# A ninth seven-product pair in half of one MLP, its operands kept in a quarter of the turned input, and one pass that adds by DMA

## The chip, the cores and the metric

The kernel runs on one core of one Trainium2 chip. The metric is the time of one execution on the device, in microseconds (us), as the median of several runs. The profile is of one further execution; its times are counted from the first instruction of its span. TensorE is called PE, its loading of the stationary operand PEld, VectorE DVE, ScalarE ACT, GpSimd POOL and SyncE SP, as in the profile.

## The reference, cut to what matters

Two layers work on 256 tokens of 2048 features in float32. The first layer mixes tokens with a convolution module, the second with latent attention; each is followed by the same kind of MLP, and a last RMSNorm ends the trunk:

```python
def sq_relu_mlp(h, w1, w2):
    return jnp.square(jax.nn.relu(h @ w1)) @ w2

for layer in range(DEPTH):
    ...
    h = rms_norm(x, norm_mlp_g[layer])
    x = x + sq_relu_mlp(h, mlp_w1[layer], mlp_w2[layer])
return rms_norm(x, final_norm_g)
```

`w1` is 2048 x 8192 and `w2` 8192 x 2048. The change is in the MLP of the first layer (`layer` 0) alone.

## The kernel before, in words

**Numbers in two parts.** Every float32 matrix is split into an upper part `hi` (a copy in float32r, by ACT) and a remainder `lo` (by DVE: the source minus `hi`), and a product is three matmuls: hi*hi, lo*hi, hi*lo (`mm3`, L202 to L204). Weights come in as tiles of 1 MB called `raw` (three buffers, loaded from SP's queue) and are split in halves of 128x1024, the upper part by L169 and the remainder by L173 for plain work, by L494 and L495 for mixed work. The results lie in tiles `hi` and `lo` with six buffers each (`WB`). So ACT and DVE can be ahead of PE by six half units of weights and no more.

**The MLP (`mlp`).** The hidden width is worked in two halves of 4096. In each half an up product makes eight groups of 512 hidden features (L650, L651, from the turned and normed input `xt`, four tiles of four 128-row blocks, each with its upper parts in one 256-column stretch and its remainders in the next). When a group's sums are complete, ACT and DVE square the rectified sums, scale them and split them into the tiles `sh`/`sl` or `gh`/`gl` (L668 to L682): two pairs of 128-row blocks a group, so 16 pairs a half, numbered 0 to 15. Then the down product runs through these 16 pairs twice, in two passes of 1024 output columns each (`for n in range(0, NNB, 2)`), into eight PSUM banks.

**Plain and mixed pairs.** A plain pair (`Sums.plain`) is a 2 x 2 block product with eight block products of three matmuls each, 24 matmuls of 512 columns. A mixed pair (`Sums.mixed`) uses the seven-product scheme of Strassen in Winograd's form, 21 matmuls, and pays for it with sums on DVE: on the weights in every pass (`mixed_weights`: L502, L503, L504 in place in `raw`, then 3584 elements a partition to split, in four pieces, instead of 2048 in two) and once on the hidden values (`mixed_inputs`, L515 to L525, into a tile of seven blocks of 128 columns for each part, called forms below). `MIXED` names the mixed pairs of each half: 0, 1, 4, 5, 8, 9, 12 and 13 in both halves of the first layer. Groups 0, 2, 4, 6 hold them, in tiles with room for seven blocks; groups 1, 3, 5, 7 are plain, in smaller tiles.

**A mixed pair in order.** PE takes block 1 of the upper weights (`b11`), `b21`, `b22`, then the summed forms `t1`, `t3`, `t4`, `t2`, three matmuls each. DVE makes the remainders of `b11` with `b21` (128x1024) and of `b22` (128x512), then L502, L503, L504, then the remainders of `t1` with `t3` and of `t4` with `t2` (128x1024 each). So the fourth product of a pair needs the third of the four pieces, and the sixth needs the last.

**The order of pairs** is set by hand in the loop over `i`: `HEAD` and `TAIL` spread the mixed pairs between the plain ones. With p for a plain pair and M for a mixed one, the first pass of the first layer's last half runs p p M M p M M p M p M M p M p p and the second p M p M p M M p M p M p M M p p. `Sums.join` adds the seven sums up before the last plain pair, and `Sums.close` adds the plain sums after it. `Sums.put` adds a finished block to the residual `xs`, on DVE (L577), or, where `by_dma` is set, through a DMA from POOL's queue that adds in place (L575); with `by_dma`, half of `close` is a copy by ACT (L601) and such a DMA too, the other half stays on DVE (L598). Before the change, `by_dma` is set in the first half of each layer and for the first pass of the second layer's last half; the first layer's last half adds all by DVE.

**Who orders the rest.** In the MLP the order of the instructions on each engine is made by the framework's planner when the kernel is built, from the program's order and its own estimate of times; the attention that follows (`manual_schedule`) keeps the order in which it is written. The first layer's last half ends in work for the next layer: in the middle of the last plain pair of its second pass, `prepare` turns the first two column blocks of `xs` into `xt[0]` and `xt[1]` (L266, L208, L215); the other two follow inside the attention.

Of the kernel before, what the change touches and what calls it, by code (L numbers as in the profile page):

```python
# [18 lines left out]
P = 128  # L19
# [3 lines left out]
S = T * P  # L23
# [18 lines left out]
WB = 6  # L42
LOOK = WB // 2 - 1
MIXED = {(layer, half): (0, 1, 4, 5, 8, 9, 12) + (13,) * (layer + half < 2) for layer in range(2) for half in range(2)}
N_MIXED = 4
HEAD, TAIL = (2, 1), 2

# [31 lines left out]
def trunk_kernel(  # L79
# [235 lines left out]
    at, cols = 0, []  # L315
# [8 lines left out]
    xt_cx, xt = [ExitStack()], []  # L324
# [184 lines left out]
    def mixed_inputs(v, fh, fl):  # L509

        def halves(src, at, n):
            hi, lo = fh[:, at : at + n, :], fl[:, at : at + n, :]
            nc.scalar.activation(hi, src, AF.Copy)  # L515
            nc.vector.tensor_tensor(lo, src, hi.bitcast(F32), op=ALU.subtract)

        a = v.rearrange("p k (t n) -> p (k t) n", t=T)
        a11, a21, a12, a22 = (a[:, i, :] for i in range(4))
        halves(a[:, 0:1, :], 0, 1)  # L520
        halves(a[:, 2:4, :], 1, 2)
        nc.vector.tensor_tensor(a22, a21, a22, op=ALU.add)
        nc.vector.tensor_tensor(a21, a11, a21, op=ALU.subtract)
        nc.vector.tensor_tensor(a11, a22, a11, op=ALU.subtract)
        nc.vector.tensor_tensor(a12, a12, a11, op=ALU.subtract)  # L525
        halves(a, 3, 4)
# [79 lines left out]
    def mlp(layer, ssq, next_gain, finish=None, before=None, beside=None, after_up=None):  # L606

        with ExitStack() as cx:
# [21 lines left out]

            for hf in range(HALVES):
                last = hf == HALVES - 1
                ms = MIXED[layer, hf]
                mixed = sorted({p // 2 for p in ms})
                plain = [g for g in range(ng) if g not in mixed]
                gs = {}
                for g in range(ng):
                    ps = [acc_tile() for _ in range(4)]
                    c0 = (hf * nkh + 4 * g) * P
                    for u in range(KC // 4):  # L640
                        if u == KC // 4 - 1:
                            step()
                        wj = load_split([rows(mlp_w1[layer], 4 * u, 4, c0, NB)], 4)
                        for j in range(4):
                            k = 4 * u + j
                            wh, wl = wj(j)
                            for b in range(4):
                                bs = slice(b * P, (b + 1) * P)

                                nc.tensor.matmul(ps[b], wh[:, bs], xhl(k), start=k == 0, stop=False)  # L650
                                nc.tensor.matmul(ps[b][:, :S], wl[:, bs], xh(k), start=False, stop=k == KC - 1)  # L651
                        step(6)
                    if hf == g == 0:
                        scales()
                    if beside is not None and g == 2:
                        beside(mp)
                        beside = None
                    if g in mixed or g in plain[len(plain) + len(mixed) - N_MIXED :]:
                        shape = [P, 2, 7, P] if g in mixed else [P, 4, S]
                        gs[g] = [mp.tile(shape, F32R, tag=f"s{c}", name=nm(f"s{c}"), bufs=N_MIXED) for c in "hl"]  # L660
                    else:
                        gs[g] = [mp.tile([P, 4, S], F32R, tag=f"g{c}", name=nm(f"g{c}"), bufs=ng - N_MIXED) for c in "hl"]
                    gh, gl = gs[g]
                    for b2 in range(2):
                        v = v_tile()
                        for b in range(2):
                            o = ps[2 * b2 + b]
                            nc.scalar.activation(v[:, b, :], o[:, S:], AF.Copy)  # L668
                            nc.vector.tensor_tensor(v[:, b, :], o[:, :S], v[:, b, :], op=ALU.add)
                        nc.vector.scalar_tensor_tensor(out=v, in0=v, scalar=0.0, in1=v, op0=ALU.max, op1=ALU.mult)  # L670
                        row = r2_row.rearrange("p (a n) -> p a n", a=1).broadcast_to([P, 2, S])
                        nc.vector.tensor_tensor(v, v, row, op=ALU.mult)
                        if 2 * g + b2 in ms:
                            mixed_inputs(v, gh[:, b2], gl[:, b2])
                            continue
                        if g in mixed:
                            v = v.rearrange("p k (t n) -> p (k t) n", t=T)
                            h, l = gh[:, b2, : 2 * T, :], gl[:, b2, : 2 * T, :]
                        else:
                            h, l = (a[:, 2 * b2 : 2 * b2 + 2, :] for a in (gh, gl))  # L680
                        nc.scalar.activation(h, v, AF.Copy)
                        nc.vector.tensor_tensor(l, v, h.bitcast(F32), op=ALU.subtract)  # L682
                nssq, add, prepare = residual_stage(last, next_gain)
                w, k_lo = mlp_w2[layer], hf * nkh
# [11 lines left out]
                due, rest = [], []  # L696

                def mixed_quad(sums, i):
                    g, b = divmod(ms[i], 2)
                    sums.mixed(w, k_lo + 4 * g + 2 * b, gs[g][0][:, b], gs[g][1][:, b], i == len(ms) - 1)  # L700

                split_end = last and finish is not None
                for n in range(0, NNB - 2 * split_end, 2):
                    sums = Sums(n, not last or split_end)
                    ks = [2 * p for p in ps]
                    at, head = 0, HEAD[n // 2]
                    for i, k in enumerate(ks):
                        upto = (len(ms) * (i - head + 1) + (head > 1) * (len(ks) - head - TAIL)) // (len(ks) - head - TAIL + 1)
                        while at < min(upto, len(ms)):
                            mixed_quad(sums, at)  # L710
                            at += 1
                        if i == len(ks) - TAIL + 1:
                            sums.join(room)
                        at_end = i == len(ks) - 1
                        sums.plain(
                            w, k_lo + k, hi, lo, k, at_end,
                            (lambda: [prepare(due.pop(0), out=room, rest=rest) for _ in range(len(due))]) if at_end else None,
                        )
                    sums.close(room)
                    while rest:  # L720
                        rest.pop(0)()
                    if last:
                        due += [n, n + 1]
                if last and not split_end:
                    put_off.extend(lambda n=n: prepare(n) for n in due)
                if split_end:
                    sums = Sums(NNB - 2, False)
# [25 lines left out]
    with ExitStack() as cx:  # L753
# [14 lines left out]
        b2 = cv.tile([P, D], F32, name="b2")  # L768
# [220 lines left out]
        with tc.manual_schedule():  # L989
# [99 lines left out]
            g = groups  # L1089
            upper_x, lower_x, last = ((0, 0),), ((0, 1),), ((1, 0),)  # L1090
# [828 lines left out]
```

## Time and profile before

| what | us |
|---|---|
| median of 3 runs (1935.26 to 1935.69) | 1935.29 |
| the profiled execution's own time | 1935.27 |
| its span, first to last instruction | 1933.5 |
| PE busy | 1919.0 |
| DVE busy | 1592.3 |
| ACT busy | 1095.5 |
| first layer, last half: up product | about 641 to 818.7 |
| its first pass of the down product | 818.7 to 900.3 |
| its second pass | 900.3 to 984.4 |

A row of the timeline gives the start, the time until the last of the merged instructions has ended, engine, line, operation, the tiles written and read, how many instructions were merged, and in brackets how long the engine sat idle before it and what ended that. Durations overlap: matmuls of 512 columns are recorded with 0.39 us each but start 0.2267 us apart (360 of them from 818.68 to 900.29). The same holds on DVE, where the next instruction starts a little before the end of the last. A wait row gives who waited for what, the sum in us, how often, and the longest.

### The profile page before, as it was taken

What the parts mean: (1) busy time and instruction counts of PE and PEld (TensorE: products, weight loads), DVE (VectorE), ACT (ScalarE), POOL (GpSimd) and SP (SyncE); (2) the same over time, 40 slices, a digit from 0 to 9 for tenths busy, and PEclk for the clock granted to TensorE, in tenths of its full rate; (3) what the DMA queues carried; (4) which work ended last, traced back from release to release, by engine and by line L of the source; (5) the groups of instructions that cost most, each with busy time, mean ns of one, the idle gap of its engine ahead of it and who ended that gap; (6) DMA issues with size and microseconds to landing.
All of it is one profiled execution on the core that took longest, in us unless ns stands there. A gap on an engine that the chain in (4) does not pass through costs nothing.

```text
span 1933.5 us, 28599 instructions
## 1 busy us (share of the span) xinstructions
PE 1919.0 (99%) x10805; PEld 1684.2 (87%) x10805; DVE 1592.3 (82%) x2464; ACT 1095.5 (57%) x1634; POOL 249.0 (13%) x208
## 2 busy tenths in 40 slices
PE   8999999999999999999999999999999999999998
PEld 8999888888888888888899998888888888888886
DVE  7999988877989777799976766877789887678898
ACT  5667755554555555555586655555555554455554
POOL 6999200000010100000001420000000010000000
PEclk9999999999999999999999999999999999999999
DMA  7766456665585866555665445465546686665674
GB/s 230 214 184 188 153 192 205 192 195 176 177 253 190 262 199 186 192 174 196 218 188 161 142 133 191 157 217 185 187 163 224 214 251 219 191 196 175 231 220 148
DMA packets 217756, 375.50 MB, mean 194 GB/s; under 512 B 16009, under 2 KB 91025, under 8 KB 217361
## 3 DMA queue, kind: packets, MB, share of 16 engines
q1 hardware_dynamic: 211968, 363.28, 58.2%
q0 software_dynamic: 4320, 7.87, 2.2%
q10 hardware_dynamic: 1328, 2.52, 0.4%
q8 instruction: 84, 1.38, 0.3%
q14 instruction: 56, 0.45, 0.1%
HBM read 363.68 MB, written 2.10 MB: 189 GB/s over the span
## 4 chain that ended last, share of the span: by engine, by line
PE 96%; DVE 2%; issue 0%; DMA 0%; ACT 0%; ACTq 0%; DVEq 0%
PE acc L650 24%; PE acc L202 15%; PE acc L204 15%; PE acc L203 15%; PE acc L651 13%; PE acc L818 8%; PE acc L1281 2%; DVE sum L905 1%; DMA xs<-in_x 0%; PE acc L1532 0%; PE acc L1555 0%; PE acc L1557 0%; PE acc L1556 0%; PE acc L1534 0%; PE acc L1533 0%
## 5 line engine op out<-in xcount | busy, mean ns | idle before, releaser
L173 DVE TENSOR_TENSOR lo<-raw,hi 128x1024 fp32r<-128x1024 f32 (+2 forms) x509 | 601.7, 1197 | 231.6 <-ACT hi L169 227.8
L169 ACT ACTIVATE hi<-raw 128x1024 fp32r<-128x1024 f32 (+2 forms) x574 | 583.9, 1036 | 358.4 <-PE acc L650 196.6
L650 PE MATMUL acc<-xt,hi 128*128 128x512 f32 x2048 | 710.5, 390 | 0.0
L651 PE MATMUL acc<-xt,lo 128*128 128x256 f32 x2048 | 577.5, 282 | 0.0
L650 PEld LDWEIGHTS acc<-xt,hi 128*128 128x128 f32 x2048 | 384.4, 188 | 80.6
L651 PEld LDWEIGHTS acc<-xt,lo 128*128 128x128 f32 x2048 | 387.1, 189 | 0.2
L494 ACT ACTIVATE hi<-raw 128x1024 fp32r<-128x1024 f32 x248 | 228.8, 949 | 234.8 <-DVE raw L502 137.6
L495 DVE TENSOR_TENSOR lo<-raw,hi 128x1024 fp32r<-128x1024 f32 x248 | 264.0, 1087 | 31.9 <-ACT hi L494 27.9
L202 PE MATMUL acc<-hi,sh 128*128 128x512 f32 x514 | 200.1, 389 | 0.0
L204 PE MATMUL acc<-lo,sh 128*128 128x512 f32 x514 | 200.1, 389 | 0.0
L202 PE MATMUL acc<-hi,gh 128*128 128x512 f32 (+1 forms) x516 | 200.0, 388 | 0.0
L203 PE MATMUL acc<-hi,gl 128*128 128x512 f32 (+1 forms) x516 | 199.9, 387 | 0.0
L204 PE MATMUL acc<-lo,gh 128*128 128x512 f32 (+1 forms) x516 | 199.9, 387 | 0.0
L818 PE MATMUL acc<-xt,hi 128*128 128x256 f32 x1024 | 180.1, 281 | 0.3 <-ACT b L1100 0.2
L203 PE MATMUL acc<-hi,sl 128*128 128x512 f32 x450 | 175.1, 389 | 0.0
L575 POOL DMA_DIRECT2D xs<-v x30 | 26.4, 972 | 1138.2 <-DVE lo L173 703.9
L905 DVE SCALAR_TENSOR_TENSOR sum<-ub,w_dw,sum 128x256 f32<-128x256 f32 x409 | 164.4, 484 | 3.5 <-ACT sum L875 3.0
L173 POOL TENSOR_TENSOR lo<-raw,hi 128x1024 fp32r<-128x1024 f32 x65 | 155.1, 2410 | 17.3 <-ACT hi L169 17.3
L818 PEld LDWEIGHTS acc<-xt,hi 128*128 128x128 f32 x1024 | 154.5, 188 | 1.1 <-ACT xt L1084 0.6
L818 PE MATMUL acc<-xt,lo 128*128 128x256 f32 x512 | 139.2, 279 | 0.0
L204 PEld LDWEIGHTS acc<-lo,sh 128*128 128x128 f32 x514 | 96.5, 188 | 20.5 <-DVE lo L495 0.3
L204 PEld LDWEIGHTS acc<-lo,gh 128*128 128x128 f32 x516 | 96.9, 188 | 19.9
(311 smaller groups left out, 2563.1 us busy)
## 6 DMA issues: line engine op xcount, KB each, us to landing
raw<-in_mlp_w SPq DMA_DIRECT2D x255, 1024.0 KB, 5.4
raw<-in_conv_w_pw SPq DMA_DIRECT2D x62, 512.0 KB, 5.0
raw<-in_conv_w_pw SPq DMA_DIRECT2D x16, 1024.0 KB, 5.0
raw<-in_mla_w_o SPq DMA_DIRECT2D x16, 1024.0 KB, 5.3
raw<-in_mla_w_kv_up SPq DMA_DIRECT2D x8, 1024.0 KB, 5.3
xs<-v POOLq DMA_DIRECT2D x30, 256.0 KB, 7.7
raw<-in_mla_w_in SPq DMA_DIRECT2D x8, 576.0 KB, 4.6
raw<-in_mla_w_in SPq DMA_DIRECT2D x4, 1024.0 KB
```

What stands on the lines that cost most here:

```text
L169: nc.scalar.activation(hi, raw[:, js, :], AF.Copy)
L173: eng.tensor_tensor(lo, raw, hi.bitcast(F32), op=ALU.subtract)
L202: nc.tensor.matmul(ps, sh, mh, start=start, stop=False)
L203: nc.tensor.matmul(ps, sl, mh, start=False, stop=False)
L204: nc.tensor.matmul(ps, sh, ml, start=False, stop=stop)
L494: nc.scalar.activation(hi, src, AF.Copy)
L495: nc.vector.tensor_tensor(lo, src, hi.bitcast(F32), op=ALU.subtract)
L650: nc.tensor.matmul(ps[b], wh[:, bs], xhl(k), start=k == 0, stop=False)
L651: nc.tensor.matmul(ps[b][:, :S], wl[:, bs], xh(k), start=False, stop=k == KC - 1)
L818: nc.tensor.matmul(pss[c][b][:, :S], w[i][:, bs], (xh, xl)[j](k), start=k == i + j == 0, stop=end and k == k0 + nk - 1 and (i, j) == terms ...
L905: nc.vector.scalar_tensor_tensor(out=out, in0=ubs[c][:, w : w + S], scalar=tap(c, w), in1=base, op0=ALU.mult, op1=ALU.add)
L1281: nc.tensor.matmul(ps2[b][t], x_kt(k, t), w[:, bs], start=k == g == i == 0, stop=k == KC - 1 and i == len(group) - 1,)
```

## The change

Pair 15 of the first layer's last half becomes a ninth mixed pair (`SPARE`). Its group, 7, has no tile with room for seven blocks, so its forms go to `xt[2]`, the quarter of the turned input that the half's up product has finished reading by then: two stretches of 896 columns. Both passes run p M p M M p M M p M M p M M p p, since `head` is 1 there. And `by_dma` is now set whenever `n == 0`, which differs from before in one place: the first pass of the first layer's last half.

```diff
+SPARE = {(0, 1): {15: 2}}
...
-                ms = MIXED[layer, hf]
+                ms, spare = MIXED[layer, hf], SPARE.get((layer, hf), {})
                 mixed = sorted({p // 2 for p in ms})
+                ms += tuple(spare)
+                forms = {}
...
-                        if 2 * g + b2 in ms:
-                            mixed_inputs(v, gh[:, b2], gl[:, b2])
+                        p = 2 * g + b2
+                        if p in spare:
+                            place = xt[spare[p]].rearrange("p a n -> p (a n)")
+                            forms[p] = [
+                                place[:, i * 4 * S : i * 4 * S + 7 * P].rearrange("p (f n) -> p f n", n=P) for i in range(2)
+                            ]
+                        elif p in ms:
+                            forms[p] = [gh[:, b2], gl[:, b2]]
+                        if p in ms:
+                            mixed_inputs(v, *forms[p])
                             continue
...
                 def mixed_quad(sums, i):
-                    g, b = divmod(ms[i], 2)
-                    sums.mixed(w, k_lo + 4 * g + 2 * b, gs[g][0][:, b], gs[g][1][:, b], i == len(ms) - 1)
+                    sums.mixed(w, k_lo + 2 * ms[i], *forms[ms[i]], i == len(ms) - 1)
...
-                    sums = Sums(n, not last or split_end)
+                    sums = Sums(n, not last or n == 0)
                     ks = [2 * p for p in ps]
-                    at, head = 0, HEAD[n // 2]
+                    at, head = 0, 1 if spare else HEAD[n // 2]
```

## The prediction

> **What bounds the kernel now.** First the page: shares of the engines, and the chain that ended last.
>
> ```profile
> span 1933.5 us, 28599 instructions
> ...
> PE 1919.0 (99%) x10805; PEld 1684.2 (87%) x10805; DVE 1592.3 (82%) x2464; ACT 1095.5 (57%) x1634; POOL 249.0 (13%) x208
> ...
> PE 96%; DVE 2%; issue 0%; DMA 0%; ACT 0%; ACTq 0%; DVEq 0%
> ```
>
> PE is never free for long, so over the whole kernel a matmul less is time less. But DVE at 82% is a mean over stages, and the change gives DVE more work in two passes. So next comes the busy time by stretches: the two passes of the first layer's first half (478 on), then those of the last half, which the change touches. The columns are the stretch, PE, PEld, DVE, ACT, POOL, the granted clock, the DMA share and GB/s.
>
> ```profile
> 478.00:560.00 82.00, 82.00 (x363) 67.90 (x363) 77.33 (x85) 45.75 (x53) 3.65 (x4) 1.00 0.60 196
> 560.00:641.00 81.00, 81.00 (x359) 67.06 (x358) 73.29 (x77) 46.10 (x51) 5.23 (x6) 1.00 0.69 219
> ...
> 818.70:900.30 81.60, 81.60 (x363) 67.58 (x362) 78.90 (x88) 45.17 (x52) 0.10 (x1) 1.00 0.56 188
> 900.30:981.80 81.50, 81.50 (x368) 67.51 (x367) 77.00 (x86) 48.04 (x62) 0.14 (x1) 1.00 0.55 189
> ```
>
> In the touched passes PE is busy throughout, and DVE for 78.9 of 81.6 us and 77.0 of 81.5. ACT has over 33 us to spare in each, the DMA engines over 40%. The waits of PE from 818 to 985 are a single row, at the start of the attention:
>
> ```profile
> PE acc L202 <- DVE xt L215: 0.4, 1, 0.4
> ```
>
> So both engines fit, with little left on DVE. How little is seen by the two timelines side by side. Mixed pairs are counted from M0 in each pass. On PE: the first matmul of the first pass, of its M2, of the plain pair after M3, and of the second pass.
>
> ```profile
> 818.68 0.39 PE L202 MATMUL acc<-hi,gh 128*128 128x512 f32 x1
> ...
> 844.53 0.39 PE L202 MATMUL acc<-hi,sh 128*128 128x512 f32 x1
> ...
> 854.05 0.39 PE L202 MATMUL acc<-hi,gh 128*128 128x512 f32 x1
> ...
> 900.29 0.39 PE L202 MATMUL acc<-hi,gh 128*128 128x512 f32 x1
> ```
>
> A pass is 8 x 21 + 8 x 24 = 360 matmuls in 81.61 us: **0.2267 us a matmul**, 5.44 a plain pair, 4.76 a mixed one (844.53 to 854.05 is two mixed: 9.52). M3 starts at 844.53 + 4.76 = 849.29 and needs t1's remainder nine matmuls later, at 851.33. On DVE at that time:
>
> ```profile
> 834.18 2.52 DVE L495 TENSOR_TENSOR lo<-raw,hi 128x1024 fp32r<-128x1024 f32 x2
> ...
> 840.62 1.22 DVE L502 TENSOR_TENSOR raw<-raw 128x1024 f32<-128x1024 f32 x1
> ...
> 847.38 1.22 DVE L502 TENSOR_TENSOR raw<-raw 128x1024 f32<-128x1024 f32 x1
> ...
> 849.97 2.52 DVE L495 TENSOR_TENSOR lo<-raw,hi 128x1024 fp32r<-128x1024 f32 x2
> ...
> 856.42 1.22 DVE L502 TENSOR_TENSOR raw<-raw 128x1024 f32<-128x1024 f32 x1
> ```
>
> The row at 849.97 is M3's last two pieces; the first ends 1.23 us on (2.52 for two that overlap), at 851.2. **The slack is 0.1 us.** And L502 to L502 is DVE's price: 840.62 to 847.38, 6.76 us for a mixed pair alone; 847.38 to 856.42, 9.04 for a mixed and a plain one, so 2.28 for the plain one. Two mixed and a plain pair cost DVE 15.80 us and PE 66 x 0.2267 = 14.96: in such a triple **DVE falls 0.84 us behind**. M1 (834.18: t1 there at 835.41, wanted at 829.57 + 4.76 + 2.04 = 836.37) had 1.0 of slack; one triple on, M3 has 0.1. The single mixed pairs between plain ones (9.04 on DVE, 45 x 0.2267 = 10.20 on PE) earn it back.
>
> **The change part by part.**
>
> *PE.* Pair 15 becomes mixed in two passes: 2 x 3 matmuls less, 6 x 0.2267 = **-1.36 us**. This is the whole direct gain. The Trainium skill ("TensorE: Matmul & The Clock Gate", Back-to-back issue gap) gives about 131 ns for a sustained matmul of 512 columns; by that it would be -0.79. The trace shows 0.2267 for float32r operands, and the measurement decides.
>
> *DVE, weights.* +6.76 - 2.28 = +4.48 us a pass, against 0.68 less of PE time.
>
> *DVE, forms.* Pair 15 gets `mixed_inputs` in place of one split. Costs by the spacing of the same instructions in group 6:
>
> ```profile
> 803.13 0.28 DVE L516 TENSOR_TENSOR sl<-v,sh 128x128 fp32r<-128x128 f32 x1
> 803.33 0.28 DVE L523 TENSOR_TENSOR v<-v 128x128 f32<-128x128 f32 x1
> 803.53 0.42 DVE L516 TENSOR_TENSOR sl<-v,sh 128x256 fp32r<-128x256 f32 x1
> 803.87 0.28 DVE L524 TENSOR_TENSOR v<-v 128x128 f32<-128x128 f32 x1
> ...
> 805.82 0.68 DVE L516 TENSOR_TENSOR sl<-v,sh 128x512 fp32r<-128x512 f32 x1
> 806.42 0.28 DVE L524 TENSOR_TENSOR v<-v 128x128 f32<-128x128 f32 x1
> ```
>
> 0.20 + 0.34 + 4 x 0.20 + 0.60 = 1.94, less the 0.60 of the 128x512 split that goes: +1.34 (by durations 2.50 - 0.68 = 1.82). It falls just ahead of the first pass, on the engine that is short. That the forms lie in `xt[2]` costs nothing: PE has read it by 818.6, before the last group's values exist, and its next writer is inside the attention.
>
> *DVE, sums.* In the first pass four puts and two of the four closing sums leave DVE: six instructions like these, 0.60 apart, **-3.6 us**, at the end of the pass. ACT gets two more copies, L601, of the size of L583's (L583's own is there already).
>
> ```profile
> 895.65 1.89 DVE L577 TENSOR_TENSOR xs<-v,xs 128x512 f32<-128x512 f32 x3
> ...
> L583 ACT ACTIVATE v<-acc 128x512 f32<-128x512 f32 x2 | 1.1, 574 | 0.0
> ...
> L575 POOL DMA_DIRECT2D xs<-v x30: 852/880/1308, 547.1 to 1846.7; - x30
> ...
>   DVE xs L598: 0.4, 1
> ...
> DMA to landing us min/median/max: 3.5/7.7/10.8
> ```
>
> POOL issues six DMAs of 256 KB, 0.88 us each; nothing else is queued on it then. The added wait: the first closing sum on DVE (L598, block 0) follows the landing of the DMA on the same block. The sum of the last plain pair but one takes PE some 10.9 us from the join, the landing 7.7 (at most 10.8), so it waits little (all 18 such sums of the trace waited 0.4 us together). Behind it on DVE would stand the next pass's weights, with slack by then (below). I take 0; bounds 0 and 1. The Trainium skill ("SBUF — State Buffer", SBUF: two separate sides) speaks against it: a DMA from GpSimd's queue has its descriptors written through a port that some DVE instructions lock, and waits until they end. Here the longest of 30 issues is 1.31 us, and the first of them run beside a DVE that is 94% busy (77.33 of 82), so the trace shows no such lock; by the rule the landing would be later, as in the rival "late adds".
>
> *The order.* M0 moves ahead of the second plain pair, so its pieces are wanted 5.44 us sooner, and the tail of the pass is a chain of four triples (p M M) instead of triples mixed with single pairs. Start of the first pass, DVE (with two ACT rows):
>
> ```profile
> 811.58 1.23 DVE L173 TENSOR_TENSOR lo<-raw,hi 128x1024 fp32r<-128x1024 f32 x1 [0.93 <-ACT hi L169]
> 814.37 1.23 DVE L173 TENSOR_TENSOR lo<-raw,hi 128x1024 fp32r<-128x1024 f32 x1 [1.56 <-ACT hi L169]
> 817.13 1.23 DVE L495 TENSOR_TENSOR lo<-raw,hi 128x1024 fp32r<-128x1024 f32 x1 [1.54 <-ACT hi L494]
> ...
> 828.71 2.96 DVE L495 TENSOR_TENSOR lo<-raw,hi 128x1024 fp32r<-128x1024 f32 x3 [1.21 <-ACT hi L494]
> ...
> 813.27 1.06 ACT L169 ACTIVATE hi<-raw 128x1024 fp32r<-128x1024 f32 x1 [1.72 <-PE acc L650]
> 816.04 1.06 ACT L494 ACTIVATE hi<-raw 128x1024 fp32r<-128x1024 f32 x1 [1.70 <-PE acc L650]
> ```
>
> Here DVE waits for ACT, and ACT for PE to free a buffer. M0's first pieces take the slots of the second plain pair (811.58 and 814.37), and L502 to L504, which need no new buffer, fit into the idle time behind them. So M0 is in time (wanted from 826.2 on), and of the 5.24 us idle in these four rows I count the last two, 1.54 + 1.21 = 2.75, as won; bounds 0 and 5.24.
>
> The balance: M2 now stands right behind M1 and wants t1 at 834.32 + 4.76 + 2.04 = 841.12. DVE has it at 835.41 + 6.76 + 1.34 - 2.75 = 840.76: slack 0.36. Three more triples cost 3 x 0.84 = 2.52, so PE waits **2.2 us** in the first pass (0 to 5.4 by the bounds, the latter with 1.82 and nothing won).
>
> Second pass: the last double today is
>
> ```profile
> 965.53 1.22 DVE L495 TENSOR_TENSOR lo<-raw,hi 128x1024 fp32r<-128x1024 f32 x1
> 966.66 0.68 DVE L504 TENSOR_TENSOR raw<-raw 128x512 f32<-128x512 f32 x1
> 968.56 1.23 DVE L495 TENSOR_TENSOR lo<-raw,hi 128x1024 fp32r<-128x1024 f32 x1 [1.21 <-ACT hi L494]
> ...
> 961.72 0.39 PE L202 MATMUL acc<-hi,sh 128*128 128x512 f32 x1
> ```
>
> PE starts the double at 961.72 and its second pair 4.76 later, wants that pair's t1 at 968.5 and has it at 966.75: 1.7 of slack. Up to this point the change takes 4.48 + 0.68 = 5.16 and gives 3.6 by the sums: 0.1 left. The last piece is only just in time already (wanted at 969.9, there at 969.79), because L504 came behind t1's remainder and DVE then waited 1.21 for ACT. I take 0.3 us of waiting; bounds 0 and 2.4 (twice 1.21).
>
> **Sum**: -1.36 + 2.2 + 0.3 = +1.1 us on the profiled execution's 1935.27, which is 0.02 below the median: **1936.4**. By the bounds -1.4 to +7.4 with the late sum's 1.
>
> **The rivals.** *DVE stays ahead.* If all idle time at the start is used, the first pass begins with over 2.5 us of slack and PE never waits: -1.36, 1933.9, no further down, as PE has no other wait there. For it: the 5.24 us idle. Against it: part of that idle is for buffers, which are as many as before. *The order of the pieces goes wrong.* The row at 968.56 shows 1.21 us of DVE idle when L504 is planned behind t1's remainder. With slack it is free; where DVE is already late it is lost. The first pass now has four doubles; if the planner does so at each, 4 x 1.21 = 4.8 comes on top: 1941.2, slower. It decides from the point where DVE's slack at M2 is under 0. Against it: at 849.97 (M3) the planner did not do so. *Late adds*: a landing of 10.8 after an issue behind another (0.9) or two holds DVE's first closing sum by 1 to 2 us, hidden by the slack between passes or not: 1936.4 to 1938. *The change does not act*, if the planner puts pair 15's forms so late that PE waits for them: the gain of 1.36 is spent there, 1935.3. Against it: pair 15 is the last mixed pair of the pass, some 65 us after its values exist.
>
> **Chances.** The forecast (waits of 1 to 4 us, so -0.4 to +2.6) 0.55; DVE stays ahead 0.27; wrong order 0.12; late adds and no effect 0.06. This kernel's measurement tells 0.2%, 3.9 us, from no change. The largest gain worked out is 1.4, so faster by more gets 0.02, for an order that changes elsewhere; slower by more gets the wrong order and a little of the forecast's tail, 0.12; the rest, 0.86, is within. The range leaves out the far part of the wrong order: 1933.8 to 1940.2.
>
> **What would show it.** Each touched pass has 357 matmuls; without waits they take 80.9 us. Right: waits of PE for DVE's L495 at the second pair of the doubles, growing along the first pass, DVE over 97% busy there, no L577 in that pass and six L575; the second pass nearly without waits. Wrong: no such waits (the first rival), DVE idle behind ACT inside the doubles (the second), or a wait of L598 for a landing.

## The result and the profile after

| kernel | median of 11 runs, us | range | ratio to before, 95% |
|---|---|---|---|
| before | 1935.4 | 1935.03 to 1936.19 | |
| changed | 1940.7 | 1939.03 to 1941.36 | 1.0025 [1.0016, 1.0035] |

The changed kernel is slower by about a quarter of a per cent. The forecast was 1936.4, and the median lies 0.5 above the top of its range. The profiled execution is the quickest of the eleven, 1939.03: on it, +3.8 us where +1.1 was forecast.

The page of the changed kernel, its first lines and the shares of the chain that ended last:

```profile
span 1937.3 us, 28629 instructions
...
PE 1920.1 (99%) x10799; PEld 1683.3 (87%) x10799; DVE 1599.0 (83%) x2474; ACT 1100.2 (57%) x1642; POOL 254.4 (13%) x214
...
PE 93%; DVE 5%; issue 1%; ACT 1%; DMA 0%; DVEq 0%; ACTq 0%
```

Six matmuls fewer, as meant, and a span 3.8 us longer. DVE's part of the chain grew from 2% to 5%. The page's mean share of DVE (82, now 83%) says nothing of this. The busy times of the two touched passes of the changed kernel do (columns as in the prediction):

```profile
819.00:901.60 82.60, 81.65 (x359) 66.86 (x358) 79.96 (x94) 48.16 (x57) 3.50 (x4) 1.00 0.61 197
901.70:984.60 82.90, 81.94 (x367) 67.03 (x366) 80.49 (x89) 50.65 (x66) 2.01 (x4) 1.00 0.63 199
```

DVE is busy for 97% of each, and PE, which was never without work here before, now has about a microsecond of gaps in each. The waits of PE in the changed kernel (who for whom, sum in us, how often, longest):

```profile
PE acc L205 <- DVE lo L496: 1.9, 4, 0.5
PE tr L267 <- DVE xt L216: 0.9, 2, 0.8
PE acc L205 <- DVE lo L174: 0.4, 1, 0.4
```

The first row is the wait that the prediction named, two in each pass. Such a wait counts from the end of the last record of 0.39 us; by the spacing of the starts each of the four costs PE 0.7 to 0.8 us. The other two rows stand at the start of the attention, where no loss was forecast.

To place the 3.8 us, both timelines of PE are cut at the same instructions: the first matmul of each pass, the first of the attention, and the first product after the attention's second set of turns.

| stretch | before | after | difference |
|---|---|---|---|
| up to the first pass | 818.68 | 819.03 | +0.35 |
| first pass | 81.61 | 82.62 | +1.01 |
| second pass, to the attention | 84.14 | 84.67 | +0.53 |
| start of the attention | 8.10 | 10.01 | +1.91 |

The sum is 3.80, and from there to the end the two timelines stay 3.8 apart. The 0.35 arises at the start of the kernel, ahead of anything that was edited. A pass now has 357 matmuls and saves 0.68; so the first pass waited 1.69 us and the second 1.21 more than before's. Before's second pass held some 0.7 us of waits itself, 0.5 of it at its end (the prediction's wait for L215, by the spacing of the starts), which the changed kernel does not have; so the changed second pass waited about 1.9 in all.

**First pass.** DVE in the changed kernel: L503 begins the sums of each mixed pair, the row at 839.38 is the last two pieces of M2, the L496 at 848.42 ends the sums of M3, the row at 856.76 is the last piece of M4, and the row at 871.26 is the two late pieces of M6.

```profile
839.38 2.52 DVE L496 TENSOR_TENSOR lo<-raw,hi 128x1024 fp32r<-128x1024 f32 x2
...
845.83 1.22 DVE L503 TENSOR_TENSOR raw<-raw 128x1024 f32<-128x1024 f32 x1
...
848.42 4.26 DVE L496 TENSOR_TENSOR lo<-raw,hi 128x1024 fp32r<-128x1024 f32 x4
...
856.76 1.23 DVE L496 TENSOR_TENSOR lo<-raw,hi 128x1024 fp32r<-128x1024 f32 x1 [0.35 <-ACT hi L495]
...
861.91 1.22 DVE L503 TENSOR_TENSOR raw<-raw 128x1024 f32<-128x1024 f32 x1
...
871.26 2.52 DVE L496 TENSOR_TENSOR lo<-raw,hi 128x1024 fp32r<-128x1024 f32 x2
...
877.70 1.22 DVE L503 TENSOR_TENSOR raw<-raw 128x1024 f32<-128x1024 f32 x1
```

861.91 to 877.70 is one triple (p M M): 15.79 us, forecast 15.80, against 14.96 for PE, and DVE has no idle time in it. The lead runs out at M6, and PE waits there and at M8. Two rows of PE's timeline after:

```profile
872.53 0.50 PE L205 MATMUL acc<-lo,sh 128*128 128x512 f32 x1 [0.51 <-DVE lo L496]
```

```profile
888.32 0.50 PE L205 MATMUL acc<-lo,xt 128*128 128x512 f32 x1 [0.44 <-DVE lo L496]
```

**Second pass.** At the turn of the passes, after: one of `join`'s sums and the last closing sum on DVE, then the next pass's first mixed weights.

```profile
893.47 0.68 DVE L587 TENSOR_TENSOR v<-acc,v 128x512 f32<-128x512 f32 x1
...
900.72 0.69 DVE L599 TENSOR_TENSOR xs<-acc,xs 128x512 f32<-128x512 f32 x1 [1.12 <-DMA xs<-v]
901.33 1.82 DVE L496 TENSOR_TENSOR lo<-raw,hi 128x1024 fp32r<-128x1024 f32 x2
```

And POOL's issue of the DMA that adds the block of L587:

```profile
894.55 0.86 POOL L576 DMA_DIRECT2D xs<-v  x1 [5.94 <-DVE v L587]
```

It lands 6.1 us after its issue, quicker than the 7.7 of the median before, and yet DVE stands idle for 1.12 us, since its closing sum on the same block was next. That is the second of the two closing sums on DVE; the first, on the block that ACT's copy feeds, did not wait. Weights for the next pass are queued behind it.

**Start of the attention.** Here the same instructions stand in another order. Before, DVE made the second of the two remainders of the attention's first weight tile (L173) between two closing sums, SP loaded the next tile into the buffer that this freed, and ACT made its upper part. Three views of before:

```profile
980.31 0.75 DVE L173 TENSOR_TENSOR lo<-raw,hi 128x576 fp32r<-128x576 f32 x1
```

```profile
981.09 0.37 SPq L1432 DMA_DIRECT2D raw<-in_mla_w_in  x1
```

```profile
986.16 0.69 ACT L169 ACTIVATE hi<-raw 128x576 fp32r<-128x576 f32 x1 [1.62 <-PE acc L203]
```

After, that remainder is the first of the four at 987.96, behind eight L216 (the six shown, two closing sums, and two more). DVE, SP, ACT and PE of the changed kernel:

```profile
983.58 2.49 DVE L216 SCALAR_TENSOR_TENSOR xt<-acc,vecs,xt 128x256 fp32r<-128x256 f32 x6
...
987.96 2.80 DVE L174 TENSOR_TENSOR lo<-raw,hi 128x576 fp32r<-128x576 f32 x4
```

```profile
988.78 0.37 SPq L1442 DMA_DIRECT2D raw<-in_mla_w_in  x1
```

```profile
992.68 0.69 ACT L170 ACTIVATE hi<-raw 128x576 fp32r<-128x576 f32 x1 [5.71 <-PE acc L204]
993.28 1.55 ACT L209 ACTIVATE xt<-tr,vecs 128x256 fp32r<-128x256 f32 x4
```

```profile
995.16 0.63 PE L267 MATMUL tr<-ident,xs 128*128 128x128 f32 x4 [0.75 <-DVE xt L216]
```

The load is issued right after the remainder in both kernels, 7.7 us later here. ACT waits 5.71 for it (the row names PE; but the load was issued 3.9 us before ACT went on, near the median of such loads on the page, here below).

```profile
raw<-in_mla_w_in SPq DMA_DIRECT2D x8, 576.0 KB, 4.4
```

ACT keeps the written order, so the copies of the turned input (L209) stand behind this wait, and PE waits for what follows from them. Of the 1.91 us, 0.62 are lost where PE waits for the late remainder itself (the L174 in its waits), before the first set of turns, and 1.29 after it.

### The profile page after: what moved, and what is told of

The parts are those of the page before. It is cut to its first block, busy times and chain, and to the rows that moved or that the text cites. A ratio compares the mean times of both kernels' runs of the same rounds, so it can differ in the third digit from the quotient of the medians.

```text
span 1937.3 us, 28629 instructions
## 1 busy us (share of the span) xinstructions
PE 1920.1 (99%) x10799; PEld 1683.3 (87%) x10799; DVE 1599.0 (83%) x2474; ACT 1100.2 (57%) x1642; POOL 254.4 (13%) x214
## 4 chain that ended last, share of the span: by engine, by line
PE 93%; DVE 5%; issue 1%; ACT 1%; DMA 0%; DVEq 0%; ACTq 0%
PE acc L653 24%; PE acc L205 14%; PE acc L203 14%; PE acc L204 14%; PE acc L654 13%; PE acc L828 8%; PE acc L1291 2%; DVE sum L915 1%; DVE lo L496 1%; DVE raw L503 0%; DVE lo L174 0%; PE acc L1542 0%; PE acc L1565 0%; PE acc L1566 0%; PE acc L1567 0%
## 5 line engine op out<-in xcount | busy, mean ns | idle before, releaser
L174 DVE TENSOR_TENSOR lo<-raw,hi 128x1024 fp32r<-128x1024 f32 (+2 forms) x505 | 597.1, 1197 | 230.0 <-ACT hi L170 226.1
L495 ACT ACTIVATE hi<-raw 128x1024 fp32r<-128x1024 f32 (+1 forms) x256 | 235.9, 949 | 234.4 <-DVE raw L503 142.6
L496 DVE TENSOR_TENSOR lo<-raw,hi 128x1024 fp32r<-128x1024 f32 (+1 forms) x256 | 272.2, 1087 | 28.9 <-ACT hi L495 24.6
L576 POOL DMA_DIRECT2D xs<-v x36 | 31.7, 973 | 1394.0 <-ACT v L584 962.6
L205 PE MATMUL acc<-lo,sh 128*128 128x512 f32 x514 | 200.5, 390 | 1.0 <-DVE lo L496 1.0
L203 PE MATMUL acc<-hi,gh 128*128 128x512 f32 (+1 forms) x500 | 193.8, 388 | 0.0
L205 PE MATMUL acc<-lo,gh 128*128 128x512 f32 (+1 forms) x500 | 193.7, 387 | 0.0
L204 PE MATMUL acc<-hi,gl 128*128 128x512 f32 (+1 forms) x500 | 193.7, 387 | 0.0
L174 POOL TENSOR_TENSOR lo<-raw,hi 128x1024 fp32r<-128x1024 f32 x65 | 155.2, 2415 | 17.6 <-ACT hi L170 17.6
L205 PEld LDWEIGHTS acc<-lo,sh 128*128 128x128 f32 x514 | 96.5, 188 | 22.7 <-DVE lo L496 2.6
L203 PEld LDWEIGHTS acc<-hi,sh 128*128 128x128 f32 x514 | 96.5, 188 | 19.8
```

What stands on the lines that cost most here:

```text
L174: eng.tensor_tensor(lo, raw, hi.bitcast(F32), op=ALU.subtract)
L203: nc.tensor.matmul(ps, sh, mh, start=start, stop=False)
L204: nc.tensor.matmul(ps, sl, mh, start=False, stop=False)
L205: nc.tensor.matmul(ps, sh, ml, start=False, stop=stop)
```

## The experiments

The standing theory at this point was the prediction's: DVE's rate in the triples is the bound. Against it stood the landing of the new DMA, the moved M0, something else in the ninth pair, and, for the help of a fourth engine, a conflict between POOL and DVE. Each run was timed in five rounds beside before (its medians there 1935.26 to 1935.51) and profiled once. Stretches are cut as above, in us; the landing column is the wait of DVE's closing sum for a DMA in the touched passes.

| run | median | ratio, 95% | first pass | second | attention | landing |
|---|---|---|---|---|---|---|
| before | 1935.4 | | 81.61 | 84.14 | 8.10 | none |
| changed | 1940.7 | 1.0016 to 1.0035 | 82.62 | 84.67 | 10.01 | 1.1 |
| e1 nine, DVE adds | 1940.9 | 1.0019 to 1.0043 | 82.72 | 85.47 | 10.47 | none |
| e2 eight, DMA adds | 1935.2 | 0.9991 to 1.0008 | 81.61 | 83.38 | 8.02 | none |
| e3 eight, M0 early | 1934.8 | 0.9990 to 1.0008 | 81.61 | 83.72 | 8.1 | none |
| e4 one pair lighter | 1938.4 | 1.0009 to 1.0027 | 82.25 | 86.20 | 8.09 | 2.6 |
| e5 single pair midway | 1938.0 | 1.0003 to 1.0020 | 82.59 | 85.26 | 8.02 | 1.7 |
| e6 nine pairs lighter | 1933.8 | 0.9985 to 1.0002 | 81.10 | 82.90 | 8.02 | none |
| e7 changed, again | 1939.5 | 1.0013 to 1.0033 | 82.59 | 85.59 | 10.05 | 2.1 |
| e8 landing avoided | 1935.9 | 0.9995 to 1.0012 | 82.74 | 83.41 | 8.1 | none |
| e9 POOL helps | 1946.8 | 1.0046 to 1.0072 | 85.81 | 90.93 | 8.23 | none |
| e10 all but the ninth | 1936.0 | 0.9994 to 1.0012 | 81.62 | 84.86 | 8.1 | none |
| e11 both passes by DMA | 1938.7 | 1.0011 to 1.0029 | 82.62 | 87.66 | 8.11 | 3.1 |
| e12 e8, lighter start | 1935.5 | 0.9992 to 1.0010 | 82.39 | 83.41 | 8.08 | none |

e2 and e3 leave the second pass's own work as it was and are 0.76 and 0.42 shorter there than before: they lack all or part of the waits that before has in its second pass. With one profile of most builds, a difference of that size in a second pass is not read.

**e1: the ninth pair, with the first pass added by DVE as before.**

```diff
-                    sums = Sums(n, not last or n == 0)
+                    sums = Sums(n, not last or split_end)
```

> The changed kernel with the sums of the first pass added by DVE again (nine mixed pairs, same order of pairs). Theory A (the ninth pair makes DVE the engine that PE waits for): DVE has six instructions of 0.60 us more, 3.6 us, at the end of the first pass; the first pass keeps its 1.7 us of waits, the second has 1.2 us plus most of the 3.6, so 1 to 3 us slower than the changed kernel, 1942 to 1944 us. Theory B (the add by DMA is the price, since DVE's first closing sums wait for its landing): the wait of 1.12 us goes and the time falls by about 1 us, to 1939.5.

It gave 1940.9, between what the two theories expected and the changed kernel's time within the interval: the second pass is 0.8 longer, the wait for a landing is gone, and the start of the attention takes 10.47. Both remainders of the attention's first weight tile stand behind the L216 here. PE loses most of the time by waiting for the second one directly; the late load is there too, and ACT's row names it, but after the first set of turns PE lost only 0.2:

```profile
PE acc L205 <- DVE lo L174: 2.0, 1, 2.0
```

```profile
993.86 0.69 ACT L170 ACTIVATE hi<-raw 128x576 fp32r<-128x576 f32 x1 [6.18 <-DMA raw<-in_mla_w_in]
```

So the DMA adds are not what made the kernel slow, and the 3.6 us that they take off DVE show in no median (1940.9 against 1940.7) and as 0.9 us in the two passes: part of what they gave went into the wait for their landing.

**e2 and e3: before, with only the DMA adds, and with only M0 moved ahead.**

```diff
-                    sums = Sums(n, not last or split_end)
+                    sums = Sums(n, not last or n == 0)
```

```diff
-                    at, head = 0, HEAD[n // 2]
+                    at, head = 0, 1 if (layer, hf) == (0, 1) else HEAD[n // 2]
```

> The kernel before with only the second half of the change: the first pass of the first layer's last half adds by DMA, eight mixed pairs in the old order. Theory A: DVE gets 3.6 us lighter where PE hardly waits, so nothing is won or lost: 1935.0 to 1935.6. Theory B: a closing sum waits 1 us or more for a landing and some of it reaches PE or the start of the attention: 1936.0 to 1937.5.

> The kernel before with only the earlier first mixed pair: the first pass of the first layer's last half takes the order of the second, p M p M p M M p M p M p M M p p, eight mixed pairs, sums by DVE. Theory A: no more work on DVE, so no more than some tenths of waits: 1935.2 to 1935.8. Rival C (the earlier place of the first mixed pair is the price, because its pieces come late): over 1 us more, from waits in the first two mixed pairs: 1936.5 or more.

Both tie with before, and PE is never idle in the touched passes (the first-pass and second-pass stretches of e2, then of e3):

```profile
819.00:901.60 82.60, 82.60 (x367) 68.40 (x366) 78.29 (x86) 46.08 (x54) 3.49 (x4) 1.00 0.61 196
901.70:984.60 82.90, 82.90 (x377) 68.95 (x377) 77.97 (x90) 51.42 (x68) 2.01 (x4) 1.00 0.63 201
```

```profile
819.00:901.60 82.60, 82.60 (x367) 68.47 (x366) 77.79 (x88) 46.74 (x54) 0.10 (x1) 1.00 0.56 191
901.70:984.60 82.90, 82.90 (x376) 68.83 (x374) 79.49 (x90) 49.92 (x66) 0.15 (x1) 1.00 0.59 192
```

Neither part costs anything alone. With DVE not short, the DMAs of e2 land in time.

**e10: everything but the ninth pair.**

```diff
-SPARE = {(0, 1): {15: 2}}
+SPARE = {}
...
-                    at, head = 0, 1 if spare else HEAD[n // 2]
+                    at, head = 0, 1 if (layer, hf) == (0, 1) else HEAD[n // 2]
```

> The changed kernel without the ninth pair: eight mixed pairs, both passes of that half in the order p M p M p M M p M p M p M M p p, the first pass adding by DMA. Theory A: DVE is 4.5 us a pass lighter than with nine, no triple follows another, so PE hardly waits and the time is that of the kernel before or some tenths less: 1934.3 to 1935.5. If the DMA or the order together cost what each alone did not, 1936 or more.

1936.0, a little above what was expected and not different from before; first pass 81.62, attention 8.1. So the loss comes with the ninth pair.

**e6: nine pairs, each with less DVE work.** L504 and L505, the last two weight sums of a pair, are left out in all nine pairs of both passes.

```diff
...
-        nc.vector.tensor_tensor(low[:, 1, :], low[:, 1, :], top[:, 0, :], op=ALU.subtract)
-        nc.vector.tensor_tensor(low[:, 0, :], low[:, 0, :], low[:, 1, :], op=ALU.subtract)
+        if sums:
+            nc.vector.tensor_tensor(low[:, 1, :], low[:, 1, :], top[:, 0, :], op=ALU.subtract)
+            nc.vector.tensor_tensor(low[:, 0, :], low[:, 0, :], low[:, 1, :], op=ALU.subtract)
...
```

> The changed kernel in which every mixed pair of the first layer's last half leaves out the second and third of its sums on the weights (L504, L505 there), so part of the product is not computed: a triple p M M costs DVE 15.8 - 2 x 1.33 = 13.1 us, less than PE's 15.0; matmuls, buffers and loads are the same. Theory A sharpened: what was lost in every triple is gone, so no waits in the doubles (under 0.3 in both passes) and none at the start of the attention: 1933.5 to 1935. Rival D (the six buffers by themselves make PE wait in the doubles, whatever DVE does): waits of 0.5 us or more stay at the second pairs of the doubles: 1937 to 1939.

Its two stretches:

```profile
819.00:901.60 82.60, 82.60 (x366) 68.25 (x365) 69.82 (x77) 47.25 (x57) 3.49 (x4) 1.00 0.64 204
901.70:984.60 82.90, 82.90 (x380) 68.99 (x380) 73.55 (x83) 52.76 (x71) 2.00 (x4) 1.00 0.65 207
```

DVE falls from 80 us to 70 and 74, and PE has no gap; 1933.8 is 1.6 below before (the interval still holds no change), PE's saving of 1.36 as near as can be told. The ninth pair's forms in `xt`, its order and its buffers make PE wait for nothing; DVE's work does. (Without these sums a piece is also ready sooner; but as DVE has no idle time in the triple above, it is the amount of its work that binds there.) The landing wait and the late attention are gone too.

**e4: the same for one pair.** The three weight sums are left out for M1 alone, once in each pass.

```diff
...
-                    sums.mixed(w, k_lo + 2 * ms[i], *forms[ms[i]], i == len(ms) - 1)
+                    sums.mixed(w, k_lo + 2 * ms[i], *forms[ms[i]], i == len(ms) - 1, not (spare and i == 1))
```

> The changed kernel in which the second mixed pair of each pass leaves out its three sums on the weights (L503 to L505 there), so part of the product is not computed: DVE has 2.6 us less in each pass, PE the same 357 matmuls. Theory A: the slack at the doubles grows by 2.6 us and the waits of 1.7 and 1.2 us go below 0.4 together; with them gone the time is 1935.4 - 1.4 plus what the start of the attention keeps (0 to 1.9): 1934.0 to 1936.3. If DVE's work is not the cause (theory B, or the start of the attention by itself), it stays at 1938.5 to 1940.5.

This missed: 1938.4 lies just below what was expected if DVE's work were not the cause, and e6 was needed to tell. Early in the pass DVE was relieved of the sums of one pair (M3's take 2.59 us in the changed kernel, 845.83 to 848.42), and the first pass waited 1.32 in place of 1.69. DVE spent the rest of the relief at once, idle behind ACT (waits of e4's DVE over both passes, and the wait for a landing, which was longer):

```profile
DVE lo L496 <- ACT hi L495: 7.4, 7, 1.8
...
DVE xs L600 <- DMA xs<-v: 2.6, 1, 2.6
```

The same wait for ACT summed to 3.5 in the changed kernel.

**e7: the changed kernel once more**, for its spread between executions.

> The changed kernel once more, for a second profile: 1939 to 1941.4. If what differs between its executions is the landing of the added DMAs, DVE's closing sum waits a different time for it than 1.12 us and the second pass differs; if it is the start of the attention (a weight load that waits for DVE to free its buffer), the time from the first matmul of the attention to the end of its second turn differs from 10.0 us.

DVE in e7, the row that answers to 900.72 above:

```profile
901.26 0.69 DVE L599 TENSOR_TENSOR xs<-acc,xs 128x512 f32<-128x512 f32 x1 [2.09 <-DMA xs<-v]
```

The same instructions in the same order: 0.97 more of waiting for the landing, and a second pass 0.92 longer. With DVE this late, a wait of its own reaches PE nearly one for one.

**e5: the second pass with its single mixed pair in the middle** (p MM p MM p M p MM p MM p p).

```diff
+                        if spare and n:
+                            upto = (0, 2, 4, 5, 7, 9, 9)[i]
```

> The changed kernel with the second pass in the order p M M p M M p M p M M p M M p p: the single mixed pair stands in the middle instead of first, so no more than two of the triples p M M follow each other. Theory A, sharpened (in each such triple DVE needs 15.8 us and PE 15.0, and the six buffers of remainders cap the lead that DVE can carry into it, so each triple after the first costs PE up to 0.84 us): the second pass's waits fall from 1.2 us to under 0.6, the first pass keeps its 1.7; if the backlog at the end of the pass falls too, so do the waits at the start of the attention: 1936.5 to 1939.5. If only the total of DVE's work counts and not the order (no cap), the second pass is unchanged and the time stays at 1939.5 to 1941.

The second pass did not get shorter, 85.26; it carried a landing wait of 1.7, so whether the order of the pairs helps there was not shown. The time lies in the range that was expected, but not by the shorter second pass that was to bring it there: the kernel is quicker than the changed one by 2.7, and its profile has 2.0 of that in the attention, 8.02: with another order in the pass, the planner put two remainders ahead of the L216 again.

**e8: no closing sum behind a DMA.** Blocks of the first column are added by DVE in `join` (some 1.2 us of DVE), so the sums of `close` on DVE touch no block that a DMA adds to.

```diff
-            self.put(0, 0, a if self.by_dma else u1)
+            self.put(0, 0, a if self.by_dma and not dve0 else u1, dve0)
...
-                self.put(t, n, o)
+                self.put(t, n, o, dve0 and n == 0)
...
-                            sums.join(room)
+                            sums.join(room, bool(spare) and n == 0)
```

> The changed kernel in which the join of the first pass adds its two blocks of the first column by DVE, and only the other two by DMA: DVE has 1.2 us more, but its closing sums touch no block that a DMA adds to. If the landing of the added DMA (1.12 and 2.09 us of DVE in two profiles) is a part of the loss by itself, the second pass's waits of PE fall by about 0 to 0.9 us and the spread between executions shrinks: 1938.5 to 1939.5. If DVE's time counts alone, 1.2 more against 1.1 to 2.1 less leaves it at 1939 to 1941. The start of the attention (1.9 us) should stay in both.

The closing sums of e8, and its second pass:

```profile
898.03 1.36 DVE L599 TENSOR_TENSOR xs<-acc,xs 128x512 f32<-128x512 f32 x2
```

```profile
901.70:984.60 82.90, 82.72 (x372) 68.06 (x370) 81.51 (x92) 51.75 (x70) 2.02 (x4) 1.00 0.62 197
```

More work for DVE (81.5 us, 98%) and fewer waits: a second pass of 83.41. In the builds in which DVE's closing sum waits for a landing (the changed kernel, e5, e7, e4) the second pass grows nearly one for one with that wait: 1.1, 1.7, 2.1 and 2.6 give 84.67, 85.26, 85.59 and 86.20 (e5's order and e4's sums differ from the others'). The time fell further than expected, to 1935.9, since the attention starts on time as well. The first pass still waits 1.81.

**e11: both passes add by DMA.**

```diff
-                    sums = Sums(n, not last or n == 0)
+                    sums = Sums(n, True)
```

> The changed kernel with the second pass adding by DMA too: DVE has 3.6 us less at the end of that pass, just before the attention. If the 1.9 us at the start of the attention come from DVE's backlog (the first attention weights' remainders late, so the buffer free late and the fourth load late), they go: 1937.0 to 1938.5, with the waits inside both passes as in the changed kernel. If the columns' landing makes the next layer's turning wait instead, 1940 or more.

The closing sum after the first pass, in e11:

```profile
904.02 0.69 DVE L599 TENSOR_TENSOR xs<-acc,xs 128x512 f32<-128x512 f32 x1 [3.10 <-DMA xs<-v]
```

The landing wait rose to 3.1 and the second pass to 87.66 (in an execution 2.7 above the median of its eleven, whose first pass began 1.3 later than the changed kernel's). The attention started on time, 8.11. As DVE has 3.6 us less to do just before it, this run alone does not tell a late DVE from a bad order; e4 and e5 do, whose second passes end later than the changed kernel's, with that pass's sums on DVE, and whose attention starts on time.

**e12: e8 with a lighter start.** ACT rectifies and squares the last group of hidden features, which takes 1.2 us off DVE at the start of the first pass.

```diff
...
-                        nc.vector.scalar_tensor_tensor(out=v, in0=v, scalar=0.0, in1=v, op0=ALU.max, op1=ALU.mult)
+                        if spare and g == ng - 1:
+                            nc.scalar.activation(v, v, AF.Relu)
+                            nc.scalar.activation(v, v, AF.Square)
+                        else:
+                            nc.vector.scalar_tensor_tensor(out=v, in0=v, scalar=0.0, in1=v, op0=ALU.max, op1=ALU.mult)
```

> The kernel without landings on DVE's blocks (the join of the first pass adds its first column by DVE) in which ACT, not DVE, rectifies and squares the last group's values: two instructions of 0.60 us less on DVE just ahead of the first pass, nothing else. If DVE's lead counts wherever it is won, the first pass's waits fall from 1.8 us by 1.2 to 0.6 and the time to 1934.6. If the six buffers cap the lead (as leaving 2.6 us out of the second mixed pair lowered the first pass's waits by 0.4 alone), the first pass keeps 1.3 to 1.8 us of waits and the time is 1935.3 to 1936.

The first pass waited 1.46, against 1.81 in e8. DVE spent the 1.2 us at once, idle behind ACT, where the same three instructions of e8 follow without a gap:

```profile
820.17 1.23 DVE L496 TENSOR_TENSOR lo<-raw,hi 128x1024 fp32r<-128x1024 f32 x1 [0.53 <-ACT hi L495]
...
822.75 1.23 DVE L174 TENSOR_TENSOR lo<-raw,hi 128x1024 fp32r<-128x1024 f32 x1 [0.42 <-ACT hi L170]
...
825.48 1.23 DVE L174 TENSOR_TENSOR lo<-raw,hi 128x1024 fp32r<-128x1024 f32 x1 [0.30 <-ACT hi L170]
```

DVE comes to the plain pair after M2 only 0.06 sooner than in e8, counted from the first matmul of the pass. The 0.35 arises later: at the last piece of M4 DVE waits 0.35 for ACT in e8, as at 856.76 in the changed kernel, and not in e12.

**e9: POOL makes the second remainder of three plain pairs a pass.**

```diff
-            at_j = split(load([rows(w, k, 2, self.n * NB, 2 * NB)], 2), nc.vector)
+            at_j = split(load([rows(w, k, 2, self.n * NB, 2 * NB)], 2), nc.vector, helper)
...
+                            nc.gpsimd if spare and 1 < i < 5 else None,
```

> The changed kernel in which POOL makes the second remainder (128x1024, 2.41 us on POOL elsewhere in the profile) of the plain pairs that stand between the doubles, three in each pass: DVE has 1.14 us less in each of these triples, 14.7 against PE's 15.0. Theory A: the waits in the doubles and at the start of the attention go and the time comes to 1934 to 1936. Rival E (POOL and DVE hold each other up while both read such tiles): DVE's or POOL's instructions get longer in these stretches and the time stays at 1938 or goes above 1941.

The slowest of all, 1946.8. A remainder on POOL in e9, and what DVE did beside it:

```profile
859.56 2.68 POOL L174 TENSOR_TENSOR lo<-raw,hi 128x1024 fp32r<-128x1024 f32 x1 [14.46 <-ACT hi L170]
```

```profile
860.47 3.46 DVE L496 TENSOR_TENSOR lo<-raw,hi 128x1024 fp32r<-128x1024 f32 x2 [0.49 <-ACT hi L495]
```

The same two pieces took DVE 1.82 in the changed kernel. POOL ends at 862.24, and 1.69 later DVE is done: it got next to nothing done in the 1.77 us beside POOL. The Trainium skill ("SBUF — State Buffer", SBUF: two separate sides) says that a DVE operation with two SBUF inputs and a GpSimd operation that reads SBUF exclude each other for the whole instruction; the rows agree.

## Why the prediction was wrong, step by step

*PE, -1.36: right.* e6, where nothing waits, gains 1.6 on before.

*DVE's price of a triple: right.* 15.79 measured.

*First pass, 2.2 of waits: right in kind, and 1.69 in size.* PE waits at the second pairs of the late doubles, as forecast, but from M6 on, where the forecast's balance has them from M4. The forecast had M2's t1 piece ready 0.36 us before it was wanted; in the changed kernel it was 1.3. Of that difference 0.45 is a misreading: the remainder of a weight enters only in the third of a product's three matmuls (PE's waits above are at L205), and the forecast counted to the first. With that corrected the sum gives 1.7. The other 0.5 is DVE earlier than forecast, and most of it goes again, 0.35, as DVE waits for ACT at M4. That the sum fits does not make slack a balance without a ceiling: ACT and DVE can be ahead by six half units and no more, so time won early is mostly spent idle behind ACT (e4: 0.4 of 2.6 us arrived; e12: 0.06 of 1.2), and only a lighter triple (e6) helps.

*"DVE, sums ... I take 0; bounds 0 and 1": this step failed first.* The closing sum waited 1.1 in one execution and 2.1 in the other, and up to 3.1 in e11. The forecast looked at block 0, which ACT's copy feeds, and set the landing against 10.9 us from the join on PE. The sum that waited is on the other block, whose DMA starts when DVE has made the join's sum, and DVE is behind by then: from the issue at 894.55 to the moment when DVE was ready for the closing sum there were 5 us. The row taken for the margin (18 closing sums, 0.4 us of waiting) was misread too: eight of the 18 are in the touched half of the kernel before, where no DMA adds, and the other ten close passes with at most eight mixed pairs. The rival "late adds" had the size, 1 to 2 us, but got less than 0.06.

*"Second pass, 0.3 us": failed with it.* 1.21 in the profiled execution. DVE enters late and the triples give nothing back, so the wait for the landing goes through (e7: 0.97 in, 0.92 out). e8, without the wait, has the second pass at 83.41. The 3.6 us credited to DVE were the right number of instructions; e1 shows that they were worth about 1 us at most.

*The attention, no term at all: the largest miss, 1.91.* The rivals had an order of the planner that goes wrong, but inside the first pass. What went wrong was the order at the end of the second pass: the second remainder of the first weight tile behind the L216 in place of ahead of them. The stretch takes 10.0 to 10.5 us in the two builds whose trace shows that order, changed (e7 is the same build) and e1, and 8.0 to 8.2 in every other build. DVE is no later at that seam than elsewhere: its first closing sum of the pass starts 4.6 to 4.7 us ahead of the attention's first matmul in before, the changed kernel, e4, e5 and e7 alike. That the late remainder causes the loss rests on this comparison and on the chain of rows above; no run moved that one instruction alone. Nor is it known why the planner chose so: e11, with a later second pass, has the good order.

*The account.* On the profiled execution the change cost 2.7 us more than forecast (3.8 against 1.1): 1.91 in the attention, 0.91 in the second pass and 0.35 at the start of the kernel, less 0.51 in the first pass, where the forecast had more.

*What stays open.* The timed median lies 1.7 above the profiled execution. e7 shows that about 1 us of it can come from the landing. Another part can come from the start of the kernel: the first pass begins anywhere from 818.48 (e8) to 820.36 (e11) in the profiles, ahead of anything edited. How much either adds to the median was not measured, and e7, the same build, has its median 1.2 lower.

No version is clearly quicker than before. e6 leaves work out; e3, e2 and e12 (1934.8 to 1935.5) tie with it.

## What to carry to other kernels

Where an engine is nearly as busy as PE in a stage (here 78.9 us of 81.6), compare its price and PE's for the repeating group of work: if the group costs it more, PE will wait at the end of the stage, and work saved once, ahead of it or early in it, is mostly lost when the buffers are full. Moving a sum to an adding DMA frees an engine only if nothing on that engine needs the same block soon, and the margin is to be counted from when the late engine will issue it, not from the plan. Where a planner orders instructions, a small edit can move others: look at the seam to the next stage, and keep a term for it.

## What the runs showed of the hardware

POOL held DVE up in e9 as told there: 2.68 us of POOL's subtraction cost DVE 1.64 (3.46 less 1.82). POOL's DMA issues were not seen to do that, nor to be held up: 0.86 us at 894.55 beside a DVE that is 97% busy, 0.88 before. The landing of an adding DMA of 256 KB was hidden in some builds and cost 1.1 to 3.1 us in others, and its wait differed by 1 us between two executions of the same build.
